# Half of the experts with float32 weights, their columns side by side on the array, and ten buffers for raw weights

## The chip, the cores and the metric

One NeuronCore of a Trainium2 chip runs the whole program. The metric is the device time of one execution in microseconds (us), lower is better; where several runs are known, the median is taken.

## What is computed

Two transformer blocks on 512 tokens of width 1024, all in float32. The part that matters here is the mixture of experts of the first block: each token goes to the 4 best of 32 experts, and each expert is three 1024x1024 matrices (4 MiB each), so 384 MiB of weights are read once.

```python
def moe(hn, router_w, router_b, w_gu, b_gu, w_down, b_down):
    ...
    logits = xt.astype(jnp.float32) @ router_w.astype(jnp.float32) + router_b.astype(jnp.float32)
    top_vals, top_idx = lax.top_k(logits, TOP_K)
    gates = jax.nn.softmax(top_vals, axis=-1)
    ...
    gu = lax.ragged_dot(xs, w_gu, group_sizes) + b_gu[sorted_e]
    gate = jnp.minimum(gu[:, ::2], SWIGLU_LIMIT)
    up = jnp.clip(gu[:, 1::2], -SWIGLU_LIMIT, SWIGLU_LIMIT)
    act = (up + 1.0) * (gate * jax.nn.sigmoid(SWIGLU_ALPHA * gate))
    y = lax.ragged_dot(act.astype(w_down.dtype), w_down, group_sizes) + b_down[sorted_e]
    y = y * gates.reshape(-1)[order][:, None].astype(y.dtype)
    out = jnp.zeros_like(xt).at[tok].add(y.astype(xt.dtype))
```

## The kernel before

`front` does the first block up to the router, `moe` the experts, `back` the rest (`embed`, then the attention of the second block). A float32 value is used as a sum of a high part of type float32r and a low part (the rest, float32r too); a product is then several float32r matmuls.

**Two kinds of experts.** `arrange` sorts the experts by their number of tokens. Sixteen with many tokens have 96 slots each (`CAP`), sixteen with few (`LESS`) have 64 (`FEW`). Tokens are gathered by an indirect DMA on POOL (`gather`, L890) and turned by TensorE (`turned`, L905). For an expert with many tokens each product takes three matmuls (`mm3`: L187, L188, L189), the low part times the low part being left out. For one with few, the high and the low part of the tokens stand side by side in one stationary operand of 128 columns, so that two matmuls do (L942: weights high, weights low); the upper 64 rows of the sum belong to the low part of the tokens. `folded` adds the two halves of rows by float32 matmuls with a 0/1 matrix (L1006).

**Weights.** `chunks` fetches 1 MiB at a time (256 rows of 1024 columns, `load`, L167, on SP's queue) into a ring of seven raw buffers (tiles wr, and h, which is two halves of a tile of the front). Per 128 rows (a k tile) ScalarE makes the high part (L937, wh<-wr) and VectorE the low part (L938, wl<-wr,wh); then TensorE multiplies. A raw buffer is free again when L938 has read it. The first seven loads, and an eighth into ys, are issued ahead (`early`, L1167).

**Order.** `stream` yields once per k tile. The experts with many tokens start alone; after 24 k tiles (`ALONE`) the two streams alternate, one k tile each, and the few end alone. Jobs (gathers, transposes, activations, scatters) are put between k tiles, some of them `LAG` tiles late. Per expert there are 4 chunks for each half of gate_up (`gate_up`) and 4 for `down`.

**Result.** `scatter` scales the sums with the gates (L1026) and adds the rows to y_d in HBM by an indirect DMA on POOL (L1028): one for an expert with many tokens, two (the upper and the lower 64 rows, each 1024 wide) for one with few. After the last one, `embed` loads y_d into h (L1265). L1051 adds the biases of gate_up by a matmul, L580, L1432 and L1556 are float32 matmuls outside the experts.

Of the kernel before, what the change touches and what calls it, by code (L numbers as in the profile page):

```python
# [12 lines left out]
I32 = mybir.dt.int32  # L13
# [12 lines left out]

FEW = 64
# [8 lines left out]
ALONE, LAG = 24, 5  # L36
# [16 lines left out]
def const_tables():  # L53
# [13 lines left out]
    t["fold"] = (p[:, None] % FEW == np.arange(FEW)[None, :]).astype(f32)  # L67
# [75 lines left out]
class Kern:  # L143
# [189 lines left out]
    def run(self):  # L333
        tc, nc, I = self.tc, self.nc, self.I
        with ExitStack() as g:
# [8 lines left out]
            with ExitStack() as a:  # L344
                wr2 = a.enter_context(tc.tile_pool(name="wr2", bufs=3))
                self.wr = [wr2, wr, wr2, wr, wr2]
                self.wh = [wh] * 2
                self.rp = a.enter_context(tc.tile_pool(name="rp", bufs=1))
                self.junk = self.rp.tile([128, D], BF16, name="junk")
                with ExitStack() as f:  # L350
                    self.front(f)
                with ExitStack() as f:
                    Q = f.enter_context(tc.tile_pool(name="mq", bufs=2, reuse_waits="tile"))
                    self.wr = [wr, wr2, wr, wr2, wr2] + [Part(self.h[:, 2 * i:2 * i + 2, :]) for i in range(2)]
                    self.moe(f, Q)
                self.wr, self.wh = [wr], [wh]
# [364 lines left out]
    def slots(self, i0, n, T, late=None):  # L721
        for t3 in self.slots_by(i0, n, T, self.tr.tile([128, 512], F32, tag="tr", name="tr"), late):
            pass
        return t3

    def slots_by(self, i0, n, T, ps, late=None):
# [31 lines left out]
        yield gi, gt  # L758
# [49 lines left out]
    def moe(self, f, Q):  # L808
        tc, nc, I, c = self.tc, self.nc, self.I, self.c
        self.psum(f, "m", 3, 1)  # L810
# [14 lines left out]
        for r in range(0, 128, NE):  # L825
            nc.scalar.dma_start(braw[r:r + NE], I["expert_b_gate_up"][0][:, r // 64 * D:r // 64 * D + D])
# [3 lines left out]
        tabs = {}  # L830
        X = {}
# [62 lines left out]
        def pair(m, tag):  # L894

            t = T.tile([128, 8, 2 * m], F32R, tag=f"{tag}{m}", name=tag)
            return t[:, :, 0:m], t[:, :, m:2 * m], t

        def turned(x, m, p):

            for j in range(2):
# [5 lines left out]
                for which in "hl":  # L907
                    self.split_in(ps, [a[:, 4 * j:4 * j + 4] for a in p[0:2]], slice(0, m), which)
                    yield 1
                free()  # L910

        def fetch(e, wait):

            while e not in tabs:
                yield 1
            gather(e)
            yield wait
            m = FEW if LESS[e] else CAP
            X[e] = pair(m, "x")
            yield from turned(xgs[LESS[e]], m, X[e])  # L920
# [3 lines left out]
        def chunks(src, ps, pair, raw=(), bias=None, few=False):  # L924


            if bias is not None and not few:
                for n in range(2):
                    bias(n, True)
            for c0 in range(0, 8, 2):  # L930
                w = raw.pop(0) if raw else self.load(src(c0 * 128, 256).rearrange("o (k p) n -> p (o k) n", p=128), 2, 1024)
                for kk in range(2):
# [6 lines left out]
                    if few:  # L939
                        for part in (hi, lo):  # L940
                            for n in range(2):
                                nc.tensor.matmul(ps[:, n, :], pair[2][:, k, :], part[:, n * 512:n * 512 + 512],  # L942
                                                 start=k == 0 and part is hi, stop=k == 7 and part is lo)
                                if bias is not None and k == 0 and part is hi:
                                    bias(n, False)
                    else:
                        for n in range(2):
                            nn = slice(n * 512, n * 512 + 512)
                            self.mm3(ps[:, n, :], (pair[0][:, k, :], pair[1][:, k, :]), (hi[:, nn], lo[:, nn]),
                                     bias is None and k == 0, k == 7)  # L950
# [16 lines left out]
        def glu(gt, up):  # L967

            def clamp(g, u):
# [3 lines left out]
                    lambda: nc.vector.scalar_tensor_tensor(out=up, in0=up, scalar=1.0, in1=gt, op0=ALU.add, op1=ALU.mult))  # L973

        def clamped(ps, half, p):
# [8 lines left out]
            mul()  # L984
# [5 lines left out]
            for which in "hl":  # L990
                self.split_in(tp, [a[:, 4 * half:4 * half + 4] for a in p[0:2]], slice(0, CAP), which)
# [3 lines left out]
        def folded(ps, half, p):  # L995


            gs = T.tile([128, 2, 512], F32, tag="gs", name="gs")
            nc.scalar.activation(gs, ps, AF.Copy)
            yield 1  # L1000
            v = gs.rearrange("p a (m s) -> p (a m) s", s=2)
            tp, free = yield from bank()
            tp = tp.rearrange("p (n m) -> p n m", n=8)
# [3 lines left out]
            yield LAG  # L1007
            gt, up = (T.tile([128, 4, FEW], F32, tag=tag, name=tag) for tag in ("ag", "au"))
            clamp, gelu, mul = glu(gt, up)
            clamp(tp[:, 0:4], tp[:, 4:8])  # L1010
            free()
            yield 1
            gelu()
            yield 1
            mul()
            yield 1
            for which in "hl":
                self.split_in(up, [a[:, 4 * half:4 * half + 4] for a in p[0:2]], slice(0, FEW), which)
                yield 1

        def scatter(ps, gate, rows, n=1):

            self.n += 1
            m = ps.shape[0]
            y = ys[0:m, self.n % 2, :]
            nc.scalar.activation(y, ps.rearrange("p a n -> p (a n)"), AF.Copy, scale=gate[0:m])  # L1026
            for o in range(0, m, m // n):
                nc.gpsimd.indirect_dma_start(out=self.y_d[:, :], out_offset=bass.IndirectOffsetOnAxis(ap=rows[0:m // n], axis=0),  # L1028
                                             in_=y[o:o + m // n], in_offset=None, bounds_check=S - 1, oob_is_err=False,
                                             compute_op=ALU.add)  # L1030
# [12 lines left out]

        def gate_up(e, half):
            few = LESS[e]
            finish(J[e, "x"])
            ps = self.mm.tile([128 if few else CAP, 2, 512], F32, tag="mm", name="mm")

            def bias(n, first):
                r = FEW if few else CAP  # L1050
                nc.tensor.matmul(ps[0:r, n, :], sel[:, half, e:e + 1].to_broadcast([128, r]),  # L1051
                                 bt[:, n * 512:n * 512 + 512], start=first, stop=False)
            ex = expert(e)
            yield from chunks(lambda r, n: wgu[ex, r:r + n, half * 1024:half * 1024 + 1024], ps, X[e], () if few else raws, bias, few)
            if half == 0:
                A[e] = pair(FEW if few else CAP, "a")
            J[e, half] = job((folded if few else clamped)(ps, half, A[e]), LAG)

        def down(e):
            few = LESS[e]  # L1060
            finish(J[e, 0])
            ps = self.mm.tile([128 if few else CAP, 2, 512], F32, tag="mm", name="mm")
# [6 lines left out]
            def out():  # L1069
                scatter(ps, tabs[e][1], tabs[e][0], 2 if few else 1)  # L1070
# [99 lines left out]
        raws = [early(i, self.next(self.wr).tile([128, 2, 1024], F32, tag="wr", name="wr")) for i in range(7)]  # L1170
        overflow()
        raws.append(early(7, ys))
# [511 lines left out]
```

## Time and profile before

| | |
|---|---|
| three runs | 1836.03, 1836.58, 1839.4 us; median 1836.58 |
| the profiled execution | 1836.86 us, of which 1835.0 us are its span |
| busy share of the span | PE 95%, DVE 83%, ACT 65%, POOL 12% |
| granted clock of TensorE | 0.981 of full speed on average |
| HBM | 470.90 MB read, 25.17 MB written |

The page of a profile has the busy time of each engine, the span in 40 slices with the share of the DMA engines and what they moved, the DMA queues, the chain of waits that ended last, and groups of like instructions. PE are TensorE's matmuls, PEld its weight loads, DVE is VectorE, ACT ScalarE, POOL GpSimd, SP the engine that issues most DMAs. A matmul is recorded as longer than the distance to the next one, since matmuls overlap; what one costs is read from the distance between starts. Names such as mm<-wh,x are output<-inputs by tile names.

### The profile page before, as it was taken

What the parts mean: (1) busy time and instruction counts of PE and PEld (TensorE: products, weight loads), DVE (VectorE), ACT (ScalarE), POOL (GpSimd) and SP (SyncE); (2) the same over time, 40 slices, a digit from 0 to 9 for tenths busy, and PEclk for the clock granted to TensorE, in tenths of its full rate; (3) what the DMA queues carried; (4) which work ended last, traced back from release to release, by engine and by line L of the source; (5) the groups of instructions that cost most, each with busy time, mean ns of one, the idle gap of its engine ahead of it and who ended that gap; (6) DMA issues with size and microseconds to landing.
All of it is one profiled execution on the core that took longest, in us unless ns stands there. A gap on an engine that the chain in (4) does not pass through costs nothing. (4 is left out here: it accounts for less than half of the span.)

```text
span 1835.0 us, 24671 instructions
## 1 busy us (share of the span) xinstructions
PE 1739.8 (95%) x8375; PEld 1285.0 (70%) x8379; DVE 1529.2 (83%) x2665; ACT 1193.9 (65%) x1591; POOL 221.2 (12%) x124
## 2 busy tenths in 40 slices
PE   8999779999999998999999999999978999999999
PEld 6887657666776775766666666766656777787776
DVE  5574589999999998999999999999977769999542
ACT  5224258778878777887788788788875445554431
POOL 0011212131111311210201211110310000000000
PEclk9999879999999998999999999999999999999999
DMA  8224469999999999999999999999985222201211
GB/s 283 85 95 149 147 219 354 384 354 389 378 391 386 373 379 363 341 391 383 379 374 393 384 371 395 383 382 391 391 291 188 91 63 82 89 28 53 84 54 40
DMA packets 148295, 493.18 MB, mean 269 GB/s; under 512 B 14369, under 2 KB 18721, under 8 KB 148160
## 3 DMA queue, kind: packets, MB, share of 16 engines
q1 hardware_dynamic: 137600, 462.02, 67.1%
q0 software_dynamic: 8640, 24.78, 6.0%
q10 hardware_dynamic: 1920, 4.72, 0.7%
q8 instruction: 68, 1.11, 0.2%
q14 instruction: 67, 0.55, 0.1%
HBM read 470.90 MB, written 25.17 MB: 270 GB/s over the span
## 5 line engine op out<-in xcount | busy, mean ns | idle before, releaser
L938 DVE TENSOR_TENSOR wl<-wr,wh 128x1024 fp32r<-128x1024 f32 x550 | 641.8, 1215 | 30.9 <-ACT wh L937 30.1
L937 ACT ACTIVATE wh<-wr 128x1024 fp32r<-128x1024 f32 x550 | 544.1, 1050 | 46.3 <-DMA wr<-in_expert_w_gate_up_dram 19.0
L938 DVE TENSOR_TENSOR wl<-h,wh 128x1024 fp32r<-128x1024 f32 x216 | 252.9, 1215 | 13.8 <-ACT wh L937 13.8
L189 PE MATMUL mm<-wl,x 128*96 128x512 f32 x512 | 208.6, 407 | 16.9 <-DVE wl L938 15.9
L937 ACT ACTIVATE wh<-h 128x1024 fp32r<-128x1024 f32 x216 | 214.9, 1050 | 14.6 <-DMA h<-in_expert_w_gate_up_dram 7.3
L187 PE MATMUL mm<-wh,x 128*96 128x512 f32 x512 | 206.0, 402 | 0.7 <-ACT x L239 0.4
L188 PE MATMUL mm<-wh,x 128*96 128x512 f32 x512 | 203.2, 397 | 0.0
L1028 POOL DMA_INDIRECT y_d<-ys,gi x48 | 116.9, 2435 | 640.5 <-ACT ys L1026 390.8
L942 PE MATMUL mm<-wl,x 128*128 128x512 f32 x512 | 169.8, 412 | 1.4 <-DVE wl L938 1.2
L942 PE MATMUL mm<-wh,x 128*128 128x512 f32 x512 | 168.1, 399 | 3.1 <-ACT wh L937 3.1
L189 PEld LDWEIGHTS mm<-wl,x 128*96 128x96 f32 x512 | 82.9, 162 | 72.5 <-DVE wl L938 41.1
L189 PE MATMUL mm<-wl,a 128*96 128x512 f32 x256 | 103.9, 406 | 15.1 <-DVE wl L938 15.0
L942 PEld LDWEIGHTS mm<-wh,x 128*128 128x128 f32 x512 | 96.2, 189 | 31.2 <-ACT wh L937 4.0
L187 PE MATMUL mm<-wh,x2h 128*128 128x512 f32 (+2 forms) x288 | 114.6, 398 | 0.3 <-ACT x2h L239 0.3
L188 PE MATMUL mm<-wh,x2l 128*128 128x512 f32 (+2 forms) x288 | 111.3, 387 | 0.0
L189 PE MATMUL mm<-wl,x2h 128*128 128x512 f32 (+2 forms) x288 | 111.0, 387 | 0.1
L942 PEld LDWEIGHTS mm<-wl,x 128*128 128x128 f32 x512 | 89.0, 189 | 29.7 <-DVE wl L938 13.2
L181 DVE TENSOR_TENSOR wl<-wr,wh 128x2048 fp32r<-128x2048 f32 (+3 forms) x40 | 76.6, 1915 | 36.7 <-ACT wh L180 36.5
L188 PEld LDWEIGHTS mm<-wh,x 128*96 128x96 f32 x512 | 83.6, 163 | 33.3 <-DVE x L241 0.4
L187 PEld LDWEIGHTS mm<-wh,x 128*96 128x96 f32 x512 | 83.2, 163 | 31.3 <-ACT wh L937 3.5
L890 POOL DMA_INDIRECT xg<-hn_d,gi x32 | 67.6, 2114 | 291.4 <-PE tr L905 229.5
L187 PE MATMUL mm<-wh,a 128*96 128x512 f32 x256 | 102.2, 399 | 0.0
(437 smaller groups left out, 3271.2 us busy)
## 6 DMA issues: line engine op xcount, KB each, us to landing
wr<-in_expert_w_gate_up_dram SPq DMA_DIRECT2D x184, 1024.0 KB, 12.6
wr<-in_expert_w_down_dram SPq DMA_DIRECT2D x91, 1024.0 KB, 13.0
h<-in_expert_w_gate_up_dram SPq DMA_DIRECT2D x71, 1024.0 KB, 11.9
h<-in_expert_w_down_dram SPq DMA_DIRECT2D x37, 1024.0 KB, 13.5
wr<-in_w_in_dram SPq DMA_DIRECT2D x20, 1024.0 KB, 5.1
wr<-in_w_out_dram SPq DMA_DIRECT2D x8, 1024.0 KB, 4.9
wr<-in_ple_gate_w_dram SPq DMA_DIRECT2D x4, 1024.0 KB, 5.3
wr<-in_w_in_dram SPq DMA_DIRECT2D x4, 512.0 KB, 5.6
```

Of the source, the lines that this page charges most:

```text
L181: nc.vector.tensor_tensor(out=lo[:, sl], in0=raw[:, sl], in1=hi[:, sl].bitcast(F32), op=ALU.subtract)
L187: mm(out, a[0], b[0], start=first, stop=False)
L188: mm(out, a[1], b[0], start=False, stop=False)
L189: mm(out, a[0], b[1], start=False, stop=last)
L890: nc.gpsimd.indirect_dma_start(out=xgs[LESS[e]][0:m], out_offset=None, in_=self.hn_d[:, :], in_offset=bass.IndirectOffsetOnAxis(ap=tabs[e] ...
L937: nc.scalar.activation(hi, w[:, kk], AF.Copy)
L938: nc.vector.tensor_tensor(out=lo, in0=w[:, kk], in1=hi.bitcast(F32), op=ALU.subtract)
L942: nc.tensor.matmul(ps[:, n, :], pair[2][:, k, :], part[:, n * 512:n * 512 + 512], start=k == 0 and part is hi, stop=k == 7 and part is lo)
L1028: nc.gpsimd.indirect_dma_start(out=self.y_d[:, :], out_offset=bass.IndirectOffsetOnAxis(ap=rows[0:m // n], axis=0), in_=y[o:o + m // n], i ...
```

## The change

For the experts with few tokens the high and low parts go: the tokens (`whole`), the activations and the weights are float32, and TensorE reads the raw buffer itself. Per k tile there are two float32 matmuls, one for columns 0 to 511 of the weights into rows 0 to 63 of the sum, one for columns 512 to 1023 into rows 64 to 127 (L961); each is placed on one half of the array's columns. The sum is one bank of PSUM instead of two (pool mf). `paired` takes the place of `folded`: no copy and no addition of halves, two transposes of 128x128. The bias takes one matmul with a selector of 128 columns. The result is 128 half rows, scattered by one DMA into y_d seen as 1024 rows of 512. The ring of raw buffers has ten places instead of seven (pool wr4), the ring of split parts four instead of six and for the experts with many tokens alone; their matmuls are ordered by part. `LAG` is 7 instead of 5.

```diff
-ALONE, LAG = 24, 5
+ALONE, LAG = 24, 7
...
-                    self.wr = [wr, wr2, wr, wr2, wr2] + [Part(self.h[:, 2 * i:2 * i + 2, :]) for i in range(2)]
+                    more = f.enter_context(tc.tile_pool(name="wr4", bufs=3, reuse_waits="tile"))
+                    self.wr = [wr, wr2, wr, wr2, wr2, more, more, more] + [Part(self.h[:, 2 * i:2 * i + 2, :]) for i in range(2)]
...
+        half = T.tile([128, n], F32, tag="sh", name="sh")
+        gh = T.tile([128, n], I32, tag="mgh", name="gh", bufs=5)
+        nc.vector.scalar_tensor_tensor(out=half, in0=v, scalar=2.0, in1=c["odd"].to_broadcast([128, n]), op0=ALU.mult, op1=ALU.add)
+        nc.vector.tensor_copy(gh, half)
+        yield gi, gt, gh
...
-        self.psum(f, "m", 3, 1)
+        self.psum(f, "m", 2, 1)
+        mf = f.enter_context(tc.tile_pool(name="mf", bufs=2, space=bass.MemoryType.PSUM))
...
-        parts += [[P.tile([128, 1024], F32R, name=f"w{k}{i}") for k in "hl"] for i in range(2)]
...
+            if m == FEW:
...
+                for i in range(8):
+                    nc.tensor.transpose(ps[:, i, :], x[0:m, i * 128:i * 128 + 128], c["ident"][0:m, 0:m])
+                yield LAG
+                nc.scalar.activation(p, ps, AF.Copy)
...
+                if few:
+                    yield c0
+                    for kk in range(2):
+                        for n in range(2):
+                            nc.tensor.matmul(ps[FEW * n:FEW * n + FEW], pair[:, c0 + kk, :], w[:, kk, n * 512:n * 512 + 512],
+                                             start=bias is None and c0 + kk == 0, stop=c0 + kk == 7)
+                    yield c0 + 1
+                    continue
...
-                    if few:
-                        for part in (hi, lo):
-                            for n in range(2):
-                                nc.tensor.matmul(ps[:, n, :], pair[2][:, k, :], part[:, n * 512:n * 512 + 512],
-                                                 start=k == 0 and part is hi, stop=k == 7 and part is lo)
...
-            gs = T.tile([128, 2, 512], F32, tag="gs", name="gs")
-            nc.scalar.activation(gs, ps, AF.Copy)
...
-            for s in range(2):
-                for b in range(4):
-                    nc.tensor.matmul(tp[:, 4 * s + b, :], v[:, b * 128:b * 128 + 128, s], c["fold"], start=True, stop=True)
...
+            for b in range(2):
+                nc.tensor.transpose(tp[:, b * 128:b * 128 + 128], up[:, b * 128:b * 128 + 128], c["ident"])
...
+            m, n = ps.shape[0], 512 if few else D
+            y = ys[0:m, self.n % 2, 0:n]
+            nc.scalar.activation(y, ps if few else ps.rearrange("p a n -> p (a n)"), AF.Copy, scale=gate[0:m])
...
+                if few:
+                    nc.tensor.matmul(ps, own[e].rearrange("p n m -> p (n m)"), row, start=True, stop=False)
...
-                scatter(ps, tabs[e][1], tabs[e][0], 2 if few else 1)
+                scatter(ps, tabs[e][1], tabs[e][2 if few else 0], few)
...
-        raws = [early(i, self.next(self.wr).tile([128, 2, 1024], F32, tag="wr", name="wr")) for i in range(7)]
+        raws = [early(i, self.next(self.wr).tile([128, 2, 1024], F32, tag="wr", name="wr")) for i in range(10)]
```

On PE, in the stretch where both streams run, two k tiles of each stood so before (96x512 are the experts with many tokens, 128x512 those with few; L187 to L189 are `mm3`):

```order
L187 MATMUL mm<-wh,x 96x512 [waits Activation_49]
L188 MATMUL mm<-wh,x 96x512
L189 MATMUL mm<-wl,x 96x512 [waits DVE_49]
...
L942 MATMUL mm<-wh_1900,x 128x512 [waits Activation_49]
L942 MATMUL mm<-wh_1900,x 128x512
L942 MATMUL mm<-wl_1901,x 128x512 [waits DVE_49]
L942 MATMUL mm<-wl_1901,x 128x512
L942 MATMUL mm<-wh,x 128x512 [waits Activation_49]
L942 MATMUL mm<-wh,x 128x512
L942 MATMUL mm<-wl,x 128x512 [waits DVE_49]
L942 MATMUL mm<-wl,x 128x512
```

and so now (L974 are those with many tokens, L961 those with few):

```order
L974 MATMUL mm<-wh,x 96x512 [waits Activation_49]
L974 MATMUL mm<-wh,x 96x512 x3
L974 MATMUL mm<-wl,x 96x512 [waits DVE_49]
L974 MATMUL mm<-wl,x 96x512
L974 MATMUL mm<-wh,x 96x512 [waits Activation_49]
L974 MATMUL mm<-wh,x 96x512 x3
L974 MATMUL mm<-wl,x 96x512 [waits DVE_49]
L974 MATMUL mm<-wl,x 96x512
L961 MATMUL mf<-wr,x 64x512 [waits DMAHW6_49]
L961 MATMUL mf<-wr,x 64x512 x3
```

A chunk of an expert with few tokens is now four matmuls of 64 rows that wait for the load itself (DMAHW), where there were eight of 128 rows that waited for ScalarE and VectorE.

On SP, the loads ahead of the experts (DVE, PE and Pool are the engines that they wait for), before:

```order
L1167 DMA wr<-in_expert_w_gate_up_dram 128x2x1024 [waits DMAHW2_49,DMAHW0_49,DVE_49]
L1167 DMA h<-in_expert_w_gate_up_dram 128x2x1024 [waits DMAHW1_49,DMAHW4_49,PE_49,DMAHW5_49,Activation_49,Pool_49]
L1167 DMA h<-in_expert_w_gate_up_dram 128x2x1024 [waits DMAHW0_49,DMAHW4_49,PE_49,DMAHW6_49,Activation_49,Pool_49]
L1121 DMA bd<-in_expert_b_down_dram 32x1024
```

and now:

```order
L1192 DMA wr<-in_expert_w_gate_up_dram 128x2x1024 [waits DMAHW2_49,DMAHW0_49,DVE_49]
L1192 DMA h<-in_expert_w_gate_up_dram 128x2x1024 [waits DMAHW1_49,DMAHW4_49,PE_49,DMAHW5_49,Activation_49,Pool_49]
L1192 DMA wr<-in_expert_w_gate_up_dram 128x2x1024 [waits DMAHW3_49]
L1192 DMA wr<-in_expert_w_gate_up_dram 128x2x1024 [waits PE_49]
L1192 DMA wr<-in_expert_w_gate_up_dram 128x2x1024 [waits DMAHW5_49]
L1192 DMA h<-in_expert_w_gate_up_dram 128x2x1024 [waits DMAHW0_49,DMAHW1_49,PE_49,DMAHW7_49,Activation_49,Pool_49]
L1146 DMA bd<-in_expert_b_down_dram 32x1024
```

The three loads more stand between the two into h, ahead of the one that waits longest.

On POOL, the scatters at the end stood so before:

```order
L890 DMA xg_1893<-hn_d,gi 64x1024
L1028 DMA y_d<-ys,gi 512x1024 x11
L1680 UNCONDITIONAL_BRANCH
```

and now:

```order
L899 DMA xg_1899<-hn_d,gi 64x1024
L1046 DMA y_d<-ys,gh 1024x512
L1046 DMA y_d<-ys,gi 512x1024
L1046 DMA y_d<-ys,gh 1024x512
L1046 DMA y_d<-ys,gi 512x1024 x2
L1046 DMA y_d<-ys,gh 1024x512 x2
L1705 UNCONDITIONAL_BRANCH
```

The last two experts end the row, with two scatters of half rows (gh) where there were four.

## Rows read from the trace of the kernel before

**Rows 1.** The page: busy times, and DMA share in slices of 45.9 us, in tenths.
```profile
PE 1739.8 (95%) x8375; PEld 1285.0 (70%) x8379; DVE 1529.2 (83%) x2665; ACT 1193.9 (65%) x1591; POOL 221.2 (12%) x124
DMA  8224469999999999999999999999985222201211
```

**Rows 2.** Stretches: from:to, us, engines' busy us (instructions), granted clock, DMA share, GB/s.
```profile
190.00:230.00 40.00, 30.31 (x180) 24.64 (x178) 22.15 (x107) 11.58 (x26) 8.79 (x14) 0.88 0.50 160
282.00:1333.00 1051.00, 1011.23 (x4691) 718.58 (x4690) 983.22 (x1167) 838.67 (x973) 175.05 (x75) 1.00 1.02 379
1300.00:1350.00 50.00, 49.34 (x229) 36.41 (x228) 46.63 (x48) 43.10 (x48) 13.28 (x3) 1.00 1.03 399
246.00:1363.00 1117.00, 1075.45 (x4985) 761.73 (x4985) 1046.12 (x1278) 889.06 (x1030) 186.24 (x80) 0.99 1.01 375
```

**Rows 3.** DMA queues (packets, MB, share of the span), then issues (median us to landing).
```profile
q1 hardware_dynamic: 137600, 462.02, 67.1%
q0 software_dynamic: 8640, 24.78, 6.0%
...
wr<-in_expert_w_gate_up_dram SPq DMA_DIRECT2D x184, 1024.0 KB, 12.6
...
wr<-in_w_in_dram SPq DMA_DIRECT2D x20, 1024.0 KB, 5.1
...
xt<-in_x_dram POOLq DMA_DIRECT2D x8, 256.0 KB, 3.1
```

**Rows 4.** Waits of SP's queue: us in total, times, longest.
```profile
SPq L167 <- DVE wl L938: 636.1, 285, 4.9
```

**Rows 5.** Groups of instructions: count, busy us, mean ns, idle before and what ended it.
```profile
L938 DVE TENSOR_TENSOR wl<-wr,wh 128x1024 fp32r<-128x1024 f32 x550 | 641.8, 1215 | 30.9 <-ACT wh L937 30.1
L938 DVE TENSOR_TENSOR wl<-h,wh 128x1024 fp32r<-128x1024 f32 x216 | 252.9, 1215 | 13.8 <-ACT wh L937 13.8
...
L1006 PE MATMUL tr<-c_small,gs 128*128 128x64 f32 x512 | 69.3, 270 | 0.0
```

**Rows 6.** Timeline of PE around 1330 us: start us, us, line.
```profile
1329.06 0.39 PE L189 MATMUL mm<-wl,a 128*96 128x512 f32 x1
1329.29 0.40 PE L187 MATMUL mm<-wh,a 128*96 128x512 f32 x1
...
1331.37 0.39 PE L942 MATMUL mm<-wh,x 128*128 128x512 f32 x1
1331.59 0.40 PE L1051 MATMUL mm<-bt,sel 128*64 128x512 f32 x1
1331.83 0.40 PE L942 MATMUL mm<-wh,x 128*128 128x512 f32 x1
```

**Rows 7.** Timeline of PE, float32 matmuls outside the experts (two records for each).
```profile
149.86 1.88 PE L580 MATMUL tr<-pooled,wp 128*128 128x512 f32 x4
...
1492.63 0.70 PE L1432 MATMUL tr<-kiT,qiT 64*128 64x256 f32 x4
...
1609.67 1.03 PE L1556 MATMUL tr<-kb,qb 100*128 100x256 f32 x4
```

**Rows 8.** Timelines of POOL and of PE at the end of the experts.
```profile
1355.11 1.68 POOL L1028 DMA_INDIRECT y_d<-ys,gi  x1 [20.65 <-ACT ys L1026]
1362.17 1.83 POOL L1028 DMA_INDIRECT y_d<-ys,gi  x1 [5.38 <-DMA y_d<-ys,gi]
1371.21 1.41 POOL L1028 DMA_INDIRECT y_d<-ys,gi  x1 [7.21 <-DMA y_d<-ys,gi]
1375.96 1.41 POOL L1028 DMA_INDIRECT y_d<-ys,gi  x1 [3.33 <-DMA y_d<-ys,gi]
...
1367.57 1.94 PE L227 MATMUL tr<-c_lasting,pt 128*128 128x128 f32 x8 [4.07 <-DMA pt<-in_p_dram]
...
1385.46 0.79 PE L187 MATMUL mm<-wph,php 128*128 128x512 f32 x1 [5.95 <-ACT pp L1646]
```

**Rows 9.** The chain that ended last, in order of time: start us, us, what.
```profile
1375.96 4.51 DMA y_d<-ys,gi
```

More of the change, by code (lines that the diff above doesn't have):

```diff
@@ L907, in turned @@
                 for which in "hl":
-                    self.split_in(ps, [a[:, 4 * j:4 * j + 4] for a in p[0:2]], slice(0, m), which)
+                    self.split_in(ps, [a[:, 4 * j:4 * j + 4] for a in p], slice(0, m), which)
                     yield 1
@@ L918, in fetch @@
             m = FEW if LESS[e] else CAP
-            X[e] = pair(m, "x")
+            X[e] = whole("x") if LESS[e] else pair(m, "x")
+            if LESS[e]:
+                own[e] = T.tile([128, 2, FEW], F32R, tag="own", name="own")
+                nc.vector.tensor_copy(own[e], sel[:, :, e:e + 1].to_broadcast([128, 2, FEW]))
             yield from turned(xgs[LESS[e]], m, X[e])
@@ L1009, in folded @@
             clamp, gelu, mul = glu(gt, up)
-            clamp(tp[:, 0:4], tp[:, 4:8])
-            free()
-            yield 1
+            clamp(gu[:, :, 0], gu[:, :, 1])
+            yield 2
             gelu()
             yield 1
[L1015 to L1021, printed above, removed]
-            self.n += 1
[L1024 to L1030, printed above, removed]
+            mul(up)
@@ new lines, in paired, with scatter @@
+            tp, free = yield from bank()
+            for b in range(2):
+                nc.tensor.transpose(tp[:, b * 128:b * 128 + 128], up[:, b * 128:b * 128 + 128], c["ident"])
+            yield LAG
+            nc.scalar.activation(p[:, 4 * half:4 * half + 4].rearrange("p (n b) m -> p b n m", b=2),
+                                 tp[:, 0:256].rearrange("p (b n m) -> p b n m", b=2, n=2), AF.Copy)
+            free()
+        y_half = self.y_d.rearrange("s (n d) -> (s n) d", n=2)
+        def scatter(ps, gate, rows, few=False):
+            self.n += 1
+            m, n = ps.shape[0], 512 if few else D
+            y = ys[0:m, self.n % 2, 0:n]
+            nc.scalar.activation(y, ps if few else ps.rearrange("p a n -> p (a n)"), AF.Copy, scale=gate[0:m])
+            nc.gpsimd.indirect_dma_start(out=y_half if few else self.y_d[:, :],
+                                         out_offset=bass.IndirectOffsetOnAxis(ap=rows[0:m], axis=0),
+                                         in_=y, in_offset=None, bounds_check=(2 if few else 1) * S - 1, oob_is_err=False,
+                                         compute_op=ALU.add)
@@ L1042, in moe, with sums @@
         J = {}
+        def sums(few):
+            return mf.tile([128, 512], F32, tag="mf", name="mf") if few else self.mm.tile([CAP, 2, 512], F32, tag="mm", name="mm")
         def gate_up(e, half):
@@ L1046, in gate_up, with bias @@
             finish(J[e, "x"])
[L1047 to L1052, printed above, removed]
+            ps = sums(few)
+            def bias():
+                row = bt[:, 512 * half:512 * half + 512]
+                if few:
+                    nc.tensor.matmul(ps, own[e].rearrange("p n m -> p (n m)"), row, start=True, stop=False)
+                else:
+                    for n in range(2):
+                        nc.tensor.matmul(ps[:, n, :], sel[:, n, e:e + 1].to_broadcast([128, CAP]), row, start=True, stop=False)
             ex = expert(e)
@@ L1055, in gate_up @@
             if half == 0:
-                A[e] = pair(FEW if few else CAP, "a")
-            J[e, half] = job((folded if few else clamped)(ps, half, A[e]), LAG)
+                A[e] = whole("a") if few else pair(CAP, "a")
+            J[e, half] = job((paired if few else clamped)(ps, half, A[e]), LAG)
         def down(e):
@@ L1061, in down @@
             finish(J[e, 0])
-            ps = self.mm.tile([128 if few else CAP, 2, 512], F32, tag="mm", name="mm")
+            ps = sums(few)
             ex = expert(e)
```

54 lines of the change are left out of this document (27 added, 27 removed).

## The prediction

> **What bounds the kernel now.** I read the slices of the span first, then stretches, then queues and waits, and the timelines last. The page shows PE busy for 95% of the span [rows 1], which would make TensorE the bound, and VectorE at 83%. The slices, however, have the DMA engines at 9 tenths or more from the seventh to the twenty-ninth, which is the stage of the experts. By stretches this stage, from the first to the last expert matmul, is 1117 us long with PE busy for 1075 us and VectorE for 1046 us; in its long middle (1051 us) the DMA share is 1.02 at 379 GB/s, so every one of the 16 DMA engines always has a packet, while the best 50 us reach 399 GB/s [rows 2]. Three resources are nearly full at once, so the reader has to see which one would stay full if another got faster. Two rows tell. A load of 1 MiB of weights lands 12.6 us after its issue, one of the same size in the front after 5.1 us [rows 3]: loads of the experts stand in a queue at the DMA engines. At 379 GB/s one MiB takes 1.049/0.379 = 2.77 us, so 12.6/2.77 = 4.5 of the seven raw buffers are in that queue, and only about 2.5 are with the engines. And SP waits 285 times, 636 us in total, for VectorE's L938 to free a buffer [rows 4]; that looks like VectorE being late, but a buffer that comes free earlier only joins the queue earlier. So the stage is bound by the DMA engines, with TensorE 4% and VectorE 6% behind. The change takes work from the engines behind and little from the one in front.
>
> **The change part by part.** *VectorE and ScalarE.* Of the 766 low parts [rows 5], 16 experts x 3 matrices x 8 k tiles = 384 go, at 1.215 us each: 467 us of VectorE, and about as much of ScalarE. Neither ends the stage, so I take nothing for it; its cover is the DMA queue, and it would be worth something only if that queue ran empty.
>
> *TensorE.* A float32r matmul of 512 columns starts 0.23 us after the one before [rows 6]. A float32 matmul appears as two records. Four records of 512 columns take 1.88 us, four of 256 columns 1.03 us [rows 7], so a column costs 0.85/1024 = 0.83 ns and a record of 512 columns 0.425 us. Now, an expert with few tokens needs 4 x 0.23 = 0.92 us per k tile (1536 matmuls, 353 us in all); after the change two float32 matmuls, four records. One after the other they take 1.70 us, in pairs side by side 0.85 us. No row of this trace has two matmuls on different column halves. The nearest has two on different row halves: the four records of L1432, whose stationary operands lie on partitions 0 to 63 and 64 to 127, take 0.70 us where four of the same width on all rows (L1556) take 1.03 us [rows 7]. Full overlap would save two starts, 0.43 us; 0.33 us are saved, and the missing 0.10 us is what a change of the array's division can cost. I take 0.85 us per k tile, 326 us in all, nearest to L1432, and keep 653 us as the other end. For going to half columns and back the bounds are nothing (L1051, a matmul of 64 columns, starts 0.22 us after its predecessor and its successor 0.24 us later [rows 6]) and 0.10 us x 192 chunks = 19 us. The 512 records of the folding, 69 us busy [rows 5], give way to 64 transposes, about 10 us by the same rows' price of 0.135 us a record; 32 of 128 bias matmuls go. Sum of TensorE's stage: before 530 (2304 x 0.23, many tokens) + 353 + 29 (bias) + 69 + 94 of other work = 1075 us as measured; after 530 + 326 + 22 + 10 + 94 = 982 us. It was behind the DMA engines and is then further behind: nothing by itself.
>
> *Scatters.* The software queue moves 24.78 MB in 6.0% of 1835 us, 110 us, or 4.4 us per MB [rows 3]. These are 6050 rows of 4 KiB. Of them 2048 are gathers (512 tokens x 4 experts), 512 rows of x in the front [rows 3], 512 the gated biases; 2978 are scatters, 2048 rows once and therefore 930 rows of the experts with few tokens a second time. After the change these 930 tokens have two half rows each: 1860 rows of 2 KiB for 1860 of 4 KiB, 3.8 MB less. At 4.4 us per MB that is 17 us of the bounding resource. Bounds: nothing, if a row costs the same whatever its length; 22 us, if gathers and x cost only what q1's bytes cost (67.1% of 1835 us for 462 MB, 2.67 us per MB), which leaves 82 us for 14.3 MB of scatters, 5.7 us per MB. I take 17.
>
> *Three more raw buffers.* The three additional loads are issued between the two into h, in a stretch where the DMA engines are busy by half only (190 to 230 us, share 0.50, that is 20 us idle [rows 2]). Three MiB at 2.77 us are 8.3 us that need not be moved later. They also take the place of an added wait: a buffer of an expert with few tokens comes free when TensorE has read it, no longer when VectorE has, and behind it on SP's queue stand the loads of both streams. With 4.5 buffers enough to keep the queue full and ten there, up to five may be with the engines. I take 8.3 us; bounds nothing (the stock is used up by a stall) and 8.3.
>
> *The end.* After the last expert's sum the two halves are scattered one behind the other, since each DMA into y_d waits for the one before: the issues are at 1355.1, 1362.2, 1371.2 and 1376.0 us [rows 8], the last one lasts 4.5 us in the chain [rows 9], and only then can y_d be loaded. Two of four go. From the last two issues 4.75 us are saved at least, and 9.0 us for the pair before if it no longer stands in the way. What is late next is the projection of the embedding: its transposes start at 1367.6 us, and PE idles 5.95 us in its middle because ScalarE waits for y_d in order [rows 8]. I take these 6 us; bounds 4.75 and 11. Larger `LAG`, the own selector (one small copy per expert) and the other order of matmuls by parts hide beside the DMA engines: nothing.
>
> Sum: 17 + 8.3 + 6 = 31 us. The profiled execution took 1836.86 us, 1835.0 us of it the span; that gives 1805.9 us, and since the median of the three runs is 0.3 us lower, **1805.5 us**.
>
> **The rivals.** *A: the column halves do not overlap.* Every record of the two halves waits for the other, as on an array that is not divided. TensorE's stage is then 982 + 326 = 1308 us, longer than the DMA engines' need, and becomes the bound: 1836.9 + (1308 - 1117) - 6 = 2022 us, slower. For it: the two halves read the same 128 partitions, while L1432's read different ones. Against: L1432 shows that float32 records of a divided array run together [rows 7]. It decides from a point: the DMA engines need (1117 - 25)/192 = 5.7 us for a pair of chunks, one of each stream. TensorE has 12 x 0.23 = 2.8 us for many tokens and 126/192 = 0.7 us of other work, so 2.2 us are left for few tokens, between 1.7 (full overlap) and 3.4 us (none): below some 70% of overlap the change loses what it gains.
>
> *B: the queue moves more once it is fuller.* The buffers are held by fewer engines and there are more of them, so the DMA engines could run at the best stretch's 399 GB/s throughout: 1051 x (1 - 379/399) = 53 us more, 1753 us. Against: the share is 1.02 already, and 399 GB/s is a stretch of 50 us [rows 2]. The Trainium skill's page "HBM Reference", section "Specifications (TRN2)", says that a core which streams alone measures about 425 GB/s; by that the DMA engines would not bind any more and the stage would last 982/0.963 = 1020 us, as TensorE was 96.3% busy, which gives about 1734 us; no stretch here shows such a rate.
>
> *C: less than the sum.* Half rows cost as much as whole ones and the stock of three MiB is lost to the first stall: only the end is gained, 1831 us.
>
> **How the numbers follow.** The sum's case has a chance of 0.66, with a range of its own from 1790 to 1824 by the bounds of its terms. A has 0.12, B 0.12, C 0.10. A change within 0.2%, 3.7 us, is about what a measurement of this kernel cannot tell from none. Faster by more: the sum's case, B and over half of C, 0.84; same: 0.04; slower: 0.12. The range of 1778 to 1832 us takes in the sum's case, C, and B where it comes out by half.
>
> **What would show it.** Right: in the stage a DMA share still at 1.0 and 375 to 385 GB/s; L938's and L937's counts 382 instead of 766; PE busy some 90 us less; the software queue at 21 MB; two scatters at the end; pairs of records on rows 0 to 63 and 64 to 127 that start within 0.02 us of each other. Wrong: records of the two halves 0.4 us apart and the DMA share well below 1 (A); a share near 1 at 395 GB/s or more (B); an unchanged time of the software queue (C). If the DMA share falls while PE idles, a wait that I have not seen took the place.

## The result, and the profile after

The changed kernel takes 1857.88 us in the median (1857.49 to 1858.63, four runs), the kernel before 1836.3 us in the same comparison: a ratio of 1.0119, 95% interval 1.0099 to 1.0139. It is 22 us slower where 31 us faster were forecast.

The page of the kernel after: busy times, DMA share and GB/s by slices, the two DMA queues, and how long a load takes to land.

```profile
PE 1709.8 (92%) x7895; PEld 1033.0 (56%) x7899; DVE 1087.1 (59%) x2255; ACT 784.9 (42%) x1159; POOL 127.1 (7%) x108
...
DMA  8224679999999999899999999999986221211211
GB/s 282 87 88 148 216 228 323 410 378 391 389 378 347 378 345 385 267 328 372 373 365 365 354 371 378 373 349 383 377 303 226 93 70 60 92 45 46 86 56 41
...
q1 hardware_dynamic: 137600, 461.99, 67.9%
q0 software_dynamic: 8384, 20.98, 4.9%
...
wr<-in_expert_w_gate_up_dram SPq DMA_DIRECT2D x206, 1024.0 KB, 9.8
```

VectorE fell from 83% to 59% and the software queue from 24.78 to 20.98 MB, as forecast. The DMA share is at 9 tenths nearly throughout as in [rows 1], but few slices now reach 391 GB/s, and a load lands after 9.8 us where it took 12.6 [rows 3]: the queue at the DMA engines has become shorter though three buffers were added. So a share of 1.0 does not show that loads end the stage.

By stretches of the kernel after (columns as in [rows 2]):

```profile
246.00:1388.00 1142.00, 1046.03 (x4504) 510.88 (x4504) 603.57 (x869) 482.15 (x600) 94.47 (x65) 0.98 0.99 360
282.00:1333.00 1051.00, 958.40 (x4112) 466.93 (x4110) 556.15 (x761) 444.80 (x556) 87.00 (x59) 0.98 1.00 364
```

The stage has grown by 25 us, 1117 to 1142. PE is idle for 96 us of it (42 before), and all engines are further from full than before. What follows the last expert matmul (1388.4 to 1855.7, 467.3 us) is 4.2 us shorter (1363.5 to 1835.0, 471.5 us).

The waits of the kernel after (engine, line, what it waited for: us in total, times, longest):

```profile
POOL y_d L1046 <- ACT ys L1045: 547.4, 18, 57.0
ACT ag L997 <- DVE ag L995: 272.2, 60, 8.6
DVE wl L971 <- ACT wh L970: 220.9, 75, 17.3
DVE ag L995 <- PE mf L961: 186.7, 29, 8.3
...
ACT ys L1045 <- PE mf L961: 131.9, 15, 11.8
...
PE mm L974 <- ACT wh L970: 28.9, 43, 1.6
...
PE mm L974 <- DVE wl L971: 27.0, 33, 1.4
```

In the stage no wait of PE for a load is among them: PE waits for high and low parts. ScalarE waits 8.8 us in all for loads of the experts, 33.9 us before. Two waits of the kernel before, VectorE's clamps for sums of experts with many tokens, then ScalarE's copies of the results of those with few:

```profile
DVE ag L970 <- PE mm L189: 12.3, 7, 1.8
...
ACT ys L1026 <- PE mm L942: 33.9, 16, 3.7
```

The second stands at the same place in the program before and after, and its wait has grown from 33.9 to 131.9 us. The clamps of the experts with many tokens now wait 18.6 us (26 times). The 186.7 us are those of the experts with few tokens, and for these the change moved the clamp: before, a copy by ScalarE, the folding and `LAG` tiles lay between the sum and the clamp, which waited 4.4 us; `paired` has it read the sum itself.

One of these places in the timelines after, VectorE first, then PE:

```profile
1187.05 4.62 DVE L971 TENSOR_TENSOR wl<-wr,wh 128x1024 fp32r<-128x1024 f32 x4
1199.73 0.42 DVE L995 TENSOR_SCALAR ag<-mf 128x256 f32<-128x256 f32 x1 [8.05 <-PE mf L961]
1200.07 0.41 DVE L996 TENSOR_SCALAR au<-mf 128x256 f32<-128x256 f32 x1
1200.40 2.35 DVE L971 TENSOR_TENSOR wl<-wr,wh 128x1024 fp32r<-128x1024 f32 x2
```

```profile
1197.18 0.63 PE L974 MATMUL mm<-wl,x 128*96 128x512 f32 x2
1197.74 1.94 PE L961 MATMUL mf<-wr,x 128*64 128x512 f32 x8
1199.61 1.16 PE L974 MATMUL mm<-wh,x 128*96 128x512 f32 x4
1201.67 0.70 PE L974 MATMUL mm<-wl,x 128*96 128x512 f32 x2 [0.90 <-DVE wl L971]
```

VectorE has made four low parts by 1191.7 us and stands for 8 us before the clamp of a sum that PE ends at 1199.7 us. The low part that PE needs next is listed behind the clamp. When the sum is done, two clamps of 0.4 us come first, and PE waits 0.90 us. The list of each engine is fixed when the program is built; in this one 56 of the 64 clamps stand straight behind the end of their sum, with no low part beyond it ahead of them, although the program lists them `LAG` tiles later. In the kernel before, this was so for 7 of the 32 clamps of the experts with many tokens, and these are the 7 that waited, 1.5 to 1.8 us each; the other 25 stood two to six low parts further back and waited for no sum.

A single larger wait lies at 740 us. POOL, then ScalarE and PE (each from its own timeline):

```profile
729.24 1.58 POOL L1046 DMA_INDIRECT y_d<-ys,gh  x1 [35.11 <-ACT ys L1045]
737.76 1.45 POOL L1046 DMA_INDIRECT y_d<-ys,gi  x1 [6.94 <-DMA y_d<-ys,gh]
747.74 1.56 POOL L1175 DMA_INDIRECT y_d<-yb,rows  x1 [8.53 <-DMA y_d<-ys,gi]
...
753.57 0.60 ACT L1173 ACTIVATE yb<-tr 128x512 f32<-128x512 f32 x1 [17.22 <-DMA y_d<-yb,rows]
...
754.22 0.80 PE L1171 MATMUL tr<-bs,gT 128*128 128x512 f32 x1 [13.53 <-ACT yb L1173]
755.16 2.02 PE L974 MATMUL mm<-wh,x 128*96 128x512 f32 x4
```

Three additions to y_d stand one behind the other, the gated biases' last; their tile yb has one place, ScalarE waits for its scatter, and PE for ScalarE. It is the slice of 267 GB/s. The stop costs more than its 13.5 us, since TensorE's granted clock fell to its lower level, 0.50, while PE was idle, and was still there for the first matmuls behind it: the four of wh at 755.16 take 2.02 us, four like them 1.16 us at 1199.61. Four microseconds of it, in the columns of [rows 2]:

```profile
752.00:756.00 4.00, 1.63 (x3) 0.96 (x4) 0.85 (x1) 2.43 (x4) 0.00 (x0) 0.50 0.24 48
```

### The profile page after: what moved, and what is told of

Same layout as the page of the kernel before. It is cut to its first block, busy times and chain, and to the rows that moved or that the text cites. A ratio compares the mean times of both kernels' runs of the same rounds, so it can differ in the third digit from the quotient of the medians.

```text
span 1855.7 us, 22422 instructions
## 1 busy us (share of the span) xinstructions
PE 1709.8 (92%) x7895; PEld 1033.0 (56%) x7899; DVE 1087.1 (59%) x2255; ACT 784.9 (42%) x1159; POOL 127.1 (7%) x108
## 3 DMA queue, kind: packets, MB, share of 16 engines
q0 software_dynamic: 8384, 20.98, 4.9%
## 5 line engine op out<-in xcount | busy, mean ns | idle before, releaser
L971 DVE TENSOR_TENSOR wl<-wr,wh 128x1024 fp32r<-128x1024 f32 x306 | 359.0, 1220 | 181.7 <-ACT wh L970 179.9
L970 ACT ACTIVATE wh<-wr 128x1024 fp32r<-128x1024 f32 x306 | 304.7, 1050 | 52.9 <-PE mm L974 30.8
L974 PE MATMUL mm<-wh,x 128*96 128x512 f32 x1024 | 296.5, 412 | 17.0 <-ACT wh L970 16.4
L974 PEld LDWEIGHTS mm<-wh,x 128*96 128x96 f32 x1024 | 161.1, 166 | 133.0 <-ACT wh L970 37.2
L961 PE MATMUL mf<-wr,x 128*64 128x512 f32 x832 | 202.7, 606 | 0.0
L974 PE MATMUL mm<-wl,x 128*96 128x512 f32 x512 | 170.7, 415 | 26.9 <-DVE wl L971 24.9
L974 PE MATMUL mm<-wh,a 128*96 128x512 f32 x512 | 143.7, 402 | 12.5 <-ACT wh L970 12.5
L974 PEld LDWEIGHTS mm<-wl,x 128*96 128x96 f32 x512 | 79.3, 166 | 84.1 <-DVE wl L971 56.5
L995 DVE TENSOR_SCALAR ag<-mf 128x256 f32<-128x256 f32 x32 | 13.6, 424 | 186.7 <-PE mf L961 186.7
L974 PEld LDWEIGHTS mm<-wh,a 128*96 128x96 f32 x512 | 77.9, 162 | 67.9 <-ACT wh L970 27.7
L971 DVE TENSOR_TENSOR wl<-h,wh 128x1024 fp32r<-128x1024 f32 x76 | 89.7, 1220 | 40.9 <-ACT wh L970 40.9
L189 PE MATMUL mm<-wh,x2l 128*128 128x512 f32 (+2 forms) x288 | 111.8, 388 | 0.0
L961 PEld LDWEIGHTS mf<-wr,x 128*64 128x64 f32 x832 | 50.9, 136 | 100.2 <-issue 96.4
L961 PE MATMUL mf<-wr,a 128*64 128x512 f32 x400 | 96.1, 604 | 0.0
L181 ACT ACTIVATE wh<-wr 128x2048 fp32r<-128x2048 f32 (+3 forms) x40 | 64.6, 1616 | 50.8 <-PE mm L189 41.1
L974 PE MATMUL mm<-wl,a 128*96 128x512 f32 x256 | 82.2, 402 | 3.6 <-DVE wl L971 2.1
L970 ACT ACTIVATE wh<-h 128x1024 fp32r<-128x1024 f32 x76 | 76.4, 1050 | 11.0 <-PE mm L974 10.5
L188 PE MATMUL mm<-wh,xh 128*128 128x512 f32 x160 | 65.8, 411 | 2.6 <-ACT xh L240 2.6
```

The costliest lines, as they stand in the source:

```text
L181: nc.scalar.activation(hi[:, sl], raw[:, sl], AF.Copy)
L188: mm(out, a[0], b[0], start=first, stop=False)
L189: mm(out, a[1], b[0], start=False, stop=False)
L961: nc.tensor.matmul(ps[FEW * n:FEW * n + FEW], pair[:, c0 + kk, :], w[:, kk, n * 512:n * 512 + 512], start=bias is None and c0 + kk == 0, s ...
L970: nc.scalar.activation(hi, w[:, kk], AF.Copy)
L971: nc.vector.tensor_tensor(out=lo, in0=w[:, kk], in1=hi.bitcast(F32), op=ALU.subtract)
```

## The experiments

The runs were made in groups, each beside the kernel before, whose median lay between 1832 and 1838 us; so a difference between runs of two groups is good to some 5 us, and where a ratio to the kernel before is given, the ratios are the better comparison. Two theories went into the first four runs. **T**: the stage has become TensorE's, by its own work. **D**: the DMA engines still end it, and are slower because raw buffers are held longer.

**Half the bytes.**

```diff
-self.load(src(c0 * 128, 256)..., 2, 1024)
+self.load(src(c0 * 128, rows)..., rows // 128, 1024)   # rows = 128 if few else 256
-pair[:, c0 + kk, :], w[:, kk, n * 512:n * 512 + 512]
+pair[:, c0 + kk, :], w[:, 0, n * 512:n * 512 + 512]
```

> The changed kernel, but each load for an expert with few tokens fetches 128 of its 256 rows, and both matmul pairs read these (the other half of those weights is left out). The DMA engines move 96 MiB less of 384, TensorE does the same. Theory T (after the change the stage belongs to TensorE: 1142 us from the first to the last expert matmul, of which 1045 us are its work and 96 us its waits for ScalarE and VectorE, with over seven loaded MiB in front of it): 1835 to 1860 us, the stage over 1120 us. Theory D (the DMA engines still end the stage, and are slower since raw buffers are held until TensorE has read them: 2.3 MiB stand in their queue instead of 4.85, 364 GB/s instead of 379): a quarter of the bytes less takes at least 80 us, 1780 us or less.

Measured: 1707.85 us in one run. T falls, in that its TensorE could do the same matmuls 150 us faster. The whole stage of that run:

```profile
246.00:1241.00 995.00, 993.06 (x4504) 511.05 (x4504) 625.12 (x869) 509.74 (x601) 91.14 (x66) 1.00 0.92 313
```

PE is busy for 993 of 995 us: that is its own need, and the 1046 us after the change hold short waits inside overlapping records and stretches at the lower clock (0.98 on average, 1.00 here). But this run doesn't prove D. With lighter loads the builder listed the engines' work in another order too: 61 of the 64 clamps now stand three or four low parts behind the end of their sum. The edit had changed two things at once.

**Half the matmuls**, all loads: `for kk in range(2)` becomes one matmul pair for each chunk.

> The changed kernel, but of each chunk of an expert with few tokens only the first 128 rows are multiplied (half of that product is left out); all loads stay. TensorE does 192 x 0.86 = 165 us less. Theory T: faster by 50 to 110 us, 1750 to 1810 us, until the DMA engines end the stage, the DMA queue then holding over 4 MiB as before the change. Theory D: within 10 us of the changed kernel's 1858 us.

Measured: 1791.53 us in one run. T's range holds, D's doesn't (less work for TensorE also helps where its waits, and not its work, make it late); loads take 17.7 us to land, so their queue is long again. About 1790 us is what the DMA engines allow.

**Seven raw buffers**: pool `more` goes, `range(10)` is `range(7)`.

> The changed kernel with seven raw buffers as before the change. Theory T: the three buffers more hold loaded weights that wait for TensorE, so within 8 us of 1858 us. Theory D: the queue at the DMA engines gets shorter still, slower by 20 us or more, 1878 us and up.

Measured: 1863.08 us in one run, 5 us more. D falls: a shorter queue would have cost far more.

**Half by half**: `for n ...: for kk ...` instead of `for kk ...: for n ...`.

> The changed kernel, but the four matmuls of a chunk of an expert with few tokens go in the order: columns 0 to 511 of both k tiles, then columns 512 to 1023 of both. If two matmuls on the array's column halves overlap only where they are neighbours in the order, one pair of four records overlaps instead of two pairs: 6 x 0.43 = 2.58 us for a chunk instead of 1.72. Theory T: TensorE has 192 x 0.86 = 165 us more, 2010 to 2035 us. Theory D: the rate of the loads hides a part of it, under 1950 us.

Measured: 1857.80 us in one run, as without the edit. Neither holds; eight records still take 1.94 us:

```profile
506.35 1.94 PE L961 MATMUL mf<-wr,a 128*64 128x512 f32 x8
```

The column halves run side by side also where the program has both k tiles of one half first.

So a third theory, **W**: the time is lost in the order. VectorE and ScalarE, with half their work, come early to copies that wait for a sum, and all parts for the next k tiles stand behind those. Against it **D2**: what TensorE gains there it loses waiting for loads.

**The bias at the end of its sum.** The matmul L1074 is issued after the last chunk, `start=False, stop=True`.

> The changed kernel, but for the experts with few tokens the matmul with the bias (L1074) ends its sum instead of starting it, so that it can't stand on TensorE's queue ahead of its bank's release. Theory W (the stage loses its time in waits of TensorE that come from the order of the instructions: VectorE's clamp L995, ScalarE's copies L997, L1034, L240 and L1045 and the bias stand just behind the end of the sum that they wait for, with no low part made ahead): the 15 pairs of waits of 0.79 and 0.45 us at L1074 go, 1836 to 1850 us. Theory D2 (the DMA engines end the stage; what TensorE waits less for one engine it waits more for loads): within 5 us of 1858.

Measured: 1867.62 us, 1.0194 of before (1.0174 to 1.0215), 10 us slower than the change (14 us by the ratios). Neither number holds. The waits of L1074 are gone, but those for wh rose from 28.9 to 43.1 us and for wl from 27.0 to 34.1 us. So a wait taken away can come back at the next copy while the order holds; what made the rest of the loss was not looked into.

**Two places for yb**: `T.tile([128, D], F32, tag="gs", name="yb")`, a tag with two buffers.

> The changed kernel with two places for the tile yb of the gated biases instead of one, so that ScalarE (L1173) needn't wait for the scatter of the one before. Theory W: the wait of 17.2 us of ScalarE and the 13.5 us of TensorE near 740 us go, 1840 to 1850 us. Theory D2: within 5 us of 1858.

Measured: 1841.57 us (1838.11 to 1847.1), 1.006 of before (1.0037 to 1.0082): 16 us come back, 11 us by the ratios.

**Copies of one column that fix the order.**

```diff
+latest[:] = hi, lo                      # after each k tile of the many
...
+nc.vector.tensor_copy(gt[:, 0:1], latest[1][0:m, 0:1])            # ahead of both clamps
+nc.scalar.activation(dst[:, 0:1], latest[0][0:m, 0:1], AF.Copy)   # ahead of x, a, ys
```

Each is overwritten by the copy that follows, which so must stand behind that part.

> The changed kernel with seven copies of one column added per pair of experts: VectorE's clamps get one from the latest low part, ScalarE's copies from PSUM (of tokens, activations and sums) one from the latest high part, so that on their engines they stand behind the parts of the k tiles that the program lists ahead of them, three or four k tiles instead of none. Loads, matmuls and buffers are the same. Theory W: nearly all waits of TensorE for wh and wl go, 1795 to 1825 us, with the DMA engines then at the end of the stage, as in the run with half the matmuls (1791.5 us). Theory D2: 1850 to 1862 us.

Measured: 1784.85 us (1779.42 to 1787.07), 0.9736 of before (0.9714 to 0.9758): 73 us less than the change (70 us by the ratios), below W's range and far from D2's. The clamps now stand four or six low parts behind the end of their sum (29 and 27 of the 64), and VectorE's wait for a sum at a clamp is 7.0 us in all. Stretches, landing of loads, and waits of this kernel:

```profile
246.00:1319.00 1073.00, 1023.98 (x4504) 508.60 (x4504) 610.42 (x933) 510.60 (x744) 95.61 (x66) 0.99 1.01 384
300.00:1280.00 980.00, 939.10 (x4127) 465.73 (x4126) 555.46 (x809) 467.05 (x679) 89.38 (x60) 0.99 1.02 391
```

```profile
wr<-in_expert_w_gate_up_dram SPq DMA_DIRECT2D x206, 1024.0 KB, 19.6
```

```profile
ACT wh L981 <- DMA wr<-in_expert_w_gate_up_dram: 183.2, 57, 6.4
ACT wh L981 <- DMA wr<-in_expert_w_down_dram: 89.8, 37, 4.8
...
ACT ag L1009 <- DVE ag L1007: 59.7, 53, 2.2
...
ACT wh L981 <- DMA h<-in_expert_w_gate_up_dram: 51.6, 15, 5.0
```

```profile
DVE ag L1007 <- PE mf L972: 7.0, 1, 7.0
```

ScalarE now waits some 340 us for loads (the three rows and 14.9 us for h<-in_expert_w_down_dram), which land 19.6 us after their issue. This is a stage bound by DMA: the wait is for the load, the queue is long, and the rate is 391 GB/s.

**The three edits together**, and two chunks of few tokens next to each other (half the changes of the array's division).

> The changed kernel with the three edits of the bias, of yb and of the copies of one column together, and the matmuls of two chunks of an expert with few tokens next to each other (half as many changes of the array's division, 0.19 us each by the distances of starts). Theory W: the end of the stage is then the DMA engines', 1780 to 1805 us, and TensorE waits for loads. Theory D2: 1845 us or more.

Measured: 1784.01 us (1782.88 to 1787.73), 0.9736 (0.972 to 0.9752): nothing beyond the copies. TensorE has time to spare there.

**Clamps alone** have their copy.

> Of the run with all copies of one column only those of VectorE's clamps (L995); ScalarE's copies from PSUM stand as in the changed kernel. Theory V (the clamps, for which VectorE waited 187 us in the changed kernel, are the place where the lead of the parts is lost): 1780 to 1800 us, as with all copies. Theory VA (ScalarE's copies of the sums, tokens and activations, for which it waited some 300 us, lose it as well): 1810 to 1845 us.

Measured: 1800.88 us (1795.7 to 1802.37), 0.9813 (0.9778 to 0.9847). This is 0.9 us above V's range and 9 us below VA's: some 57 of the 73 us are the clamps', 16 us ScalarE's copies.

Three runs on the kernel with all copies, where DMA does end the stage, priced the forecast's terms. **Seven buffers** in it:

> The kernel with all copies of one column and seven raw buffers instead of ten. By the forecast's term the stock of three MiB is worth up to 8.3 us: 1785 to 1794 us. Theory S (now that the loads end the stage and raw buffers are held until TensorE has read them, seven are too few to keep the DMA engines supplied): 1800 us or more.

Measured: 1787.18 us (1784.31 to 1791.63): 2.3 us, within the spread of either. S falls.

**Each scatter of half rows twice**:

> The kernel with all copies of one column, but each scatter of half rows is issued twice (the sums of the experts with few tokens are added twice): 1860 half rows, 3.8 MB, more, just what the change saved by the forecast's term. By that term 17 us more, bounds 0 and 22: 1785 to 1807 us, likeliest 1802 less what the second scatter adds at the end of the stage (some 5 us), so 1807 at most 1812. Theory N (half rows cost as much as whole ones, or nothing, and the DMA engines' rate comes from elsewhere): within 4 us of 1785 apart from the 5 us at the end.

Measured: 1810.78 us (1807.62 to 1814.42), 26 us more. The last expert matmul ends at 1335.8 instead of 1318.6 us, 17.2 us later, and 9 us lie behind it. The software queue takes 6.2% of 1808.5 us, 112 us, for 90.9 us without. The term of 17 us holds; what I added for the end was too little. N's range falls. The run adds rows and bytes alike, so it rules out that half rows cost nothing; that they cost less than whole ones is shown by the queue's time before and after the change, for as many rows.

**Two places for yb** in it:

> The kernel with all copies of one column and two places for yb. If loads end the stage nothing is gained: 1780 to 1788 us. If the wait for the scatter of yb still stops the loads near 740 us, where their rate was 371 GB/s in one slice instead of 390: 1772 to 1780 us.

Measured: 1784.14 us (1783.17 to 1787.9): nothing, as DMA ends the stage.

The last three runs asked whether the order was a burden before, and which edit displaced the clamps.

**The kernel before with such copies**:

> The kernel before the change with the same copies of one column ahead of its clamps (L970) and its copies from PSUM (L999, L1026, the high parts of tokens and activations). Theory B (before the change VectorE, 94% busy, came to its clamps after the sum was done, waiting 12 us for them in all, so their place in the order cost little; it costs since VectorE has half its work and arrives early): within 8 us of the kernel before, 1825 to 1843 us. Theory O (the order cost as much before): faster by 20 us or more, 1815 us or less.

Measured: 1840.55 us (1836.23 to 1842.76), 1.0029 (1.0017 to 1.0042). B holds: there the copies only cost.

**The change with `LAG` 5**:

> The changed kernel with LAG 5 as before the change. Theory L (the larger LAG, by which the program lists the copies two k tiles later, is what displaced them): 1835 us or less. Theory W (the clamps stand just behind their sum whatever LAG is, since VectorE's order of instructions is the same with either): within 8 us of 1858 us.

Measured: 1836.86 us (1830.62 to 1843.01), 1.0014 (1.0001 to 1.0028). Neither theory had it: 21 us go, but not through the clamps, which stand as before the edit and wait as long:

```profile
DVE ag L995 <- PE mf L961: 183.3, 30, 8.3
...
PE mm L974 <- ACT wh L970: 27.8, 42, 1.5
PE mm L974 <- DVE wl L971: 27.6, 34, 1.3
```

What is missing from PE's waits is the one of 13.5 us at L1171: with the smaller lag the gated biases' scatters fall beside the others. The granted clock is at 1.00 from 740 to 800 us, where it was 0.86, so the 21 us can be more than the wait itself.

**Six pairs of parts, eight raw buffers**:

> The changed kernel with a ring of six pairs of parts as before the change, and eight raw buffers instead of ten to make room. Theory R (four pairs are too few for a lead): 1835 us or less. Theory W (the lead is lost by the order, not by the room): 1850 to 1868 us.

Measured: 1856.64 us (1854.17 to 1864.01), 1.0121 (1.0091 to 1.0151). R falls: 58 of the 64 clamps stand straight behind their sum, and those of few tokens wait as long as before the edit (187.5 us).

## Why the prediction was wrong

**The step that failed** is the second sentence on VectorE and ScalarE: "Neither ends the stage, so I take nothing for it; its cover is the DMA queue". An engine with less work isn't only idle more: what it waits for next, and what is listed behind that wait, comes to matter. Before, most clamps had low parts ahead of them in the list, or stood behind the folding, and VectorE, 94% busy in the stage, waited 16.7 us at them in all. After, 56 of 64 stand straight behind their sum, and VectorE, with 384 low parts gone, has made all parts ahead of them early: it waits 187 us at the clamps of few tokens alone, ScalarE waits 272 us behind it, and the low part that TensorE needs next is behind the clamp. TensorE then consumes more slowly than loads arrive. The copies show that the order costs this: with no change in loads, matmuls or buffers they give back 73 us, while they give nothing in the kernel before. How much of it is VectorE's and ScalarE's relief, and how much that `paired` put the clamp directly on the sum, no run separates; that the relief has a part is likely, since ScalarE's wait grew also at its copies of the results, whose place in the program did not change (33.9 to 131.9 us). I had named the sign ("If the DMA share falls while PE idles"), yet but for the stop at 740 us (0.87 from there to 800 us) the share stayed at 1.0; the time to landing is what fell. The Trainium skill's page "Perfetto Trace Analysis", section "Identifying the Most-Contended Engine", says that with 16 DMA engines their occupancy misleads; this trace agrees, with a share of 1.00 at 364 GB/s and no wait of PE for a load in the stage.

**The second step** is "Larger `LAG`, the own selector ... and the other order of matmuls by parts hide beside the DMA engines: nothing". For `LAG` it fails: with 5 the change takes 21 us less (19 us by the ratios), and two places for yb give 16 us (11 us); both remove the one wait at 740 us. That the wait falls just there is an accident of which scatters meet. It makes the difference between a change of no measurable effect and a slower one. The other two edits were not tried by themselves.

**TensorE's sum** came out: 982 us were forecast, 993 us measured where nothing waits. The halves overlap as I took from L1432, four pairs 0.43 us apart in the 1.94 us above. The change of the array's division was priced too low: L961 to the next L974 takes 1.87 us (1197.74 to 1199.61) where four pairs need 1.72, and the two matmuls ahead of it 0.56 us where 0.47 is usual (1353.84 to 1354.31 in the rows below, which are PE's timeline after), some 0.24 us for a chunk against my bound of 0.10. That is 46 us which the sum of 982 us leaves out, so the rest of it was too high by some 35 us. Rival A did not happen: the overlap is full.

```profile
1353.84 0.64 PE L974 MATMUL mm<-wl,a 128*96 128x512 f32 x2
1354.31 1.09 PE L974 MATMUL mm<-wh,a 128*96 128x512 f32 x4
```

**Scatters**: the queue's time fell from 110 to 91 us (4.9% of 1855.7), 19 us where I had taken 17, and doubled scatters of half rows delay the last matmul by 17.2 us. Right, but hidden in a stage that DMA didn't end. **Three buffers**: 8.3 us forecast; 5 us in one run of the change, 2.3 us where DMA binds. The stock of three MiB is of little use; the lower bound was the better value. **The end**: 4.2 us for 6, just below my bound of 4.75.

**The range**: with the order mended the kernel takes 1784.85 us, 21 us below the forecast of the sum. Rival B had a part in that: 391 GB/s instead of 379, for 399 in its text. So the loads did not bind the stage before as fully as I took from its share of 1.02: a load landed after 12.6 us and ScalarE waited 33.9 us for loads, for 19.6 and 340 us with the order mended. The range of the sum's case is not the one that its terms' bounds give, either: these give 1795 to 1832 us, not 1790 to 1824. The rival that was missing is the one that came: an early engine that stops at a wait, with the critical work listed behind it. The rows had a sign of it: without the 467 us of [rows 5] VectorE would be idle for over 40% of the stage, and an engine that is early has to stand at some wait.

What stays open is why the builder put the clamps there: its choice was seen (two parts and more for 25 of 32 before, no lead after with full loads, three or four parts with half of them), not its reason.

## What to carry to other kernels

Before costing relief of an engine at nothing, look in its instruction list for the next wait that it will reach early, and for what another engine needs that stands behind it; a one-column copy that makes the waiting instruction depend on later work moves it, and was worth some 70 us here. A DMA share of 1.0 doesn't show that loads are the bound: the time from issue to landing and the waits that name a DMA do. A single-place tile behind a chain of scatters turned a shift of a few microseconds elsewhere into a stop of TensorE, and of most loads with it (48 GB/s from 752 to 756 us).

## What the runs showed of the hardware that I had not expected

Float32 matmuls on the two column halves overlap fully while both read the same 128 partitions, and also when a half's two matmuls are listed together (eight records in 1.94 us either way). One core's loads held 391 GB/s over 980 us, with ScalarE waiting for them, where the stage before, with some 4.5 MiB in the queue, had 379 GB/s. The Trainium skill's page "HBM Reference", section "Specifications (TRN2)", gives about 425 GB/s for a core that streams alone; no run here held that. And TensorE's busy time doesn't show how much of it is work: 1046 us were recorded for what took 993 us in the run with half the bytes. Part of the difference are short waits, which the records cover (a matmul of 0.39 us where starts are 0.23 us apart), part the lower granted clock (0.98 for 1.00); no run separates the two.
